# A hybrid SSM and attention encoder layer in fp32: two buffers and five renormalisations of its state stage changed

## The chip, the cores and the metric

The kernel runs as one program on one core of one Trainium2 chip. Its time is the device time of one execution, in microseconds (us); the kernel before took 918.15 us, the median of 3 executions (916.77 to 918.69). In the text PE is TensorE (matmuls and transposes), DVE is VectorE, ACT is ScalarE, POOL is GpSimd, and SP is the engine whose queue issues most DMAs. Each engine works through its own list of instructions in order; a semaphore holds an instruction back until what it needs is there.

## What is computed

One layer of an encoder for 512 tokens of width 1024, with 16 learned meta tokens in front, so L = 528 rows. All of it is float32.

```
h = rms_norm(x);  u, q, k, v, g_ssm, g_attn = split(h @ W_in)      # 512 | 1024 | 256 | 256 | 1024 | 1024
y = D * u + sum over 2 directions of Re(C x),  x[l] = lam * x[l-1] + B u[l]
                                         # 32 groups of 16 channels, 64 complex states in each
z = gelu(y);  y_ssm = z * sigmoid(z @ W_glu + b)
y_attn = attention(rope(rms_norm(q)), rope(rms_norm(k)), v)         # 16 heads, 4 KV heads
x = x + W_out(sigmoid(g_ssm) * (y_ssm @ P_ssm) + sigmoid(g_attn) * (y_attn @ P_attn))
x = x + relu(rms_norm(x) @ W1)^2 @ W2;   out = rms_norm(x)[16:]
```

`lam` = exp((a_re + i a_im) dt) is one complex number for each of 2 x 32 x 64 states. Its modulus and its phase are kept apart: the scan uses the modulus, and the phases are put on and taken off by complex rotations.

## The kernel before

Every fp32 matmul is done as three products of fp32r halves (`mm3`, L159 to L161: high by high, low by high, high by low). A weight arrives by DMA (`wf`), ACT casts it to its high half (`wh`, L98), and DVE subtracts to get the low half (`wl`, L125). PE takes 128 x 512 tiles of these products out of PSUM accumulators.

The program has stages. The first 60 us or so make the norm of x, k and v, and the small tables of the SSM on DVE (tiles `p`, 128 x 32). The **state stage** follows, from about 60 to 236 us of the span; the change lies in it alone. Behind it come the norm of k (L916 to L937), the half-GLU (L1042), attention with its query projections, the merge, W_out, and the MLP, which is by far the largest part.

The state stage treats the 32 groups in 8 runs of 4 groups, in 8-step blocks (66 columns). Directions share the partitions: 0 to 63 forward, 64 to 127 backward. Each run i has a generator `ssm_build(i)` and a generator `ssm_run(i)`:

- `ssm_build`: DVE makes the input matrices W1 (L711 to L713), PE transposes them (L720), ACT copies them out (L721). DVE makes the output matrices W2 (L728 to L733, two buffers each; the last PE reader of a buffer is the matmul `yo`, L815). The phases of the columns are the products `x1`, `x2` (L747, twice) and their sum `e` (L749); ACT copies their imaginary part as `es` (L751, L752). Then PE multiplies `kt` (L758), ACT takes most of it out (L762, L763), DVE the middle (L764, L765), and DMAs lay out the local matrix T0 (L769).
- `phase_tables`, called once in the first build that needs it, makes the powers of the phase step by doubling: a complex product (L560 to L565), then the next step is squared (`csq`) and brought back to modulus one (`renorm`: six DVE operations on 128 x 32). Three doublings serve the table of 8 entries, four that of 9.
- `ssm_run`: PE multiplies the inputs by W1 (`st`, L787), ACT copies the sums into the tile `Sx` (L789, L790), DVE rotates (L795 to L797), scans along the columns (L800, into Sx again), and rotates back; the second L797 is the last step ahead of the states. ACT copies the states into `X` (L806, L807), and PE finishes with `yo` (L813 from T0, L815 from X). After two runs PE transposes (`yt`) and ACT takes the GELU.

Two temporaries, rs1 (a piece of `gbuf`) and rs2, serve both the phase products of a build (`x1`, `x2`) and the rotations of a run (`m1`, `m2`); `Sx` is one buffer. So a build's L747 may not write rs1 before ACT has copied the states of the run before out of it (L807), and the next run's copies into Sx may not begin before the last rotation has read it.

Between the parts of these generators `pump` puts tiles of the gate projection (`gps`) and of u (`ups`) into PE's list as filler: matmuls that need none of the states. A gate tile is 24 matmuls of 128 x 512. `ssm_in` transposes u into the blocks (`up`, L672; Vc, L98; `ug`, L678; Uf, L679). The code is written in generator order, and a scheduler that simulates a timeline then fixes one order per engine, with the priorities of its own estimate; the order of the instructions is thus a result of the whole program, and an edit at one place can move instructions at another.

Of the kernel before, what the change touches and what calls it, by code (L numbers as in the profile page):

```python
# [10 lines left out]
F32 = mybir.dt.float32  # L11
# [59 lines left out]
def hybrid_block(ctx, tc, x, meta, w_in, w_glu, w_ssm, w_attn, w_out, w_m1, w_m2,  # L71
# [3 lines left out]
    V, S, Q, PE = nc.vector, nc.scalar, nc.gpsimd, nc.tensor  # L75
# [110 lines left out]
    yfl = ybuf.rearrange("p k n -> p (k n)")  # L186
# [36 lines left out]
    def ptile(pl=None, shape=(128, G), dt=F32):  # L223
        cnt[0] += 1
        return (pl or pp).tile(list(shape), dt, name=f"p{cnt[0]}")
# [269 lines left out]
    def ts(a, s1, op0, s2=None, op1=None, o=None):  # L495
        o = ptile() if o is None else o
        if op1 is None:
            V.tensor_scalar(out=o, in0=a, scalar1=s1, scalar2=None, op0=op0)
        else:
            V.tensor_scalar(out=o, in0=a, scalar1=s1, scalar2=s2, op0=op0, op1=op1)  # L500
        return o

    def stt(a, s, b, op0, op1, o=None):
        o = ptile() if o is None else o
        V.scalar_tensor_tensor(out=o, in0=a, scalar=s, in1=b, op0=op0, op1=op1)
        return o
# [52 lines left out]
    def cmul(eng, orr, oi, ar, ai, br, bi, t1_, t2_):  # L559
        eng.tensor_tensor(out=t1_, in0=ar, in1=br, op=ALU.mult)  # L560
        eng.tensor_tensor(out=t2_, in0=ai, in1=bi, op=ALU.mult)
        eng.tensor_tensor(out=orr, in0=t1_, in1=t2_, op=ALU.subtract)
        eng.tensor_tensor(out=t1_, in0=ar, in1=bi, op=ALU.mult)
        eng.tensor_tensor(out=t2_, in0=ai, in1=br, op=ALU.mult)
        eng.tensor_tensor(out=oi, in0=t1_, in1=t2_, op=ALU.add)  # L565
# [5 lines left out]
    def tz(a, b, op):  # L571
        return tt(a, b, op, o=ptile(ppz))

    def csq(r, i):
        rr = tz(tz(r, r, ALU.mult), tz(i, i, ALU.mult), ALU.subtract)
        ii = stt(r, 2.0, i, ALU.mult, ALU.mult, o=ptile(ppz))
        return rr, ii

    def renorm(r, i):
        m = tz(tz(r, r, ALU.mult), tz(i, i, ALU.mult), ALU.add)  # L580
        m = ts(m, -0.5, ALU.mult, 1.5, ALU.add, o=ptile(ppz))
        return tz(r, m, ALU.mult), tz(i, m, ALU.mult)

    wr, wi = cs, sn
    for _ in range(3):
        wr, wi = csq(wr, wi)
    wr, wi = renorm(wr, wi)
    wri = wr, wi

    def phase_tables():  # L590
        wr, wi = wri
        phase = []
        for nb in (8, 9):
            tr_ = sp.tile([128, G, nb], F32, name=f"ph{nb}r")
            ti_ = sp.tile([128, G, nb], F32, name=f"ph{nb}i")
            V.memset(tr_[:, :, 0:1], 1.0)
            V.memset(ti_[:, :, 0:1], 0.0)
            m = 1
            while m < nb:
                n = min(m, nb - m)  # L600
                bcw = [a[:, :, None].to_broadcast([128, G, n]) for a in (wr, wi)]
                s1, s2 = [a[:, :G * n].rearrange("p (g n) -> p g n", g=G) for a in (sc5, sc6)]
                cmul(V, tr_[:, :, m:m + n], ti_[:, :, m:m + n], tr_[:, :, 0:n], ti_[:, :, 0:n], bcw[0], bcw[1], s1, s2)
                m *= 2
                if m < nb or nb == 8:
                    wr, wi = renorm(*csq(wr, wi))
            phase.append((tr_, ti_))

        (pbr, pbi), (par, pai) = phase
        pa1, pa2 = [sp.tile([128, G, 2, 9], F32, name=f"pa{j}") for j in range(2)]  # L610
        S.copy(out=pa1[:, :, 0], in_=par)
        S.copy(out=pa1[:, :, 1], in_=pai)
        S.activation(out=pa2[:, :, 0], in_=pai, func=AF.Copy, scale=-1.0)
        S.copy(out=pa2[:, :, 1], in_=par)
        return pa1, pa2, pbr, pbi
# [46 lines left out]
    sw = pool(ss_st, "sw")  # L662
# [28 lines left out]
    rs1, rs2 = gfl[:, 1536:2112], sp.tile([128, 576], F32, name="rs2")  # L691
# [3 lines left out]
    def ssm_build(i8):  # L695

        gs = slice(4 * i8, 4 * i8 + 4)

        def bp(a):
            return a[:, gs, :, None].to_broadcast(W4)  # L700

        def bb(a):
            return a[:, gs, None, :].to_broadcast(W4)

        tmp = [yfl[:, 512 * j:512 * j + 512].rearrange("p (g s q) -> p g s q", g=4, s=T) for j in range(8)]

        W1T = []
        for im in range(2):
            tB, tC, tA = tmp[0], tmp[1], tmp[2 + im]
            a0, a1 = (LBr, LBi) if im == 0 else (LBi, LBr)  # L710
            V.tensor_tensor(out=tB, in0=bb(a0), in1=bp(PA[0]), op=ALU.mult)  # L711
            V.tensor_tensor(out=tC, in0=bb(a1), in1=bp(PA[1]), op=ALU.mult)
            V.tensor_tensor(out=tA[:, :, ::-1, :], in0=tB, in1=tC, op=ALU.subtract if im == 0 else ALU.add)  # L713
        yield
        for im in range(2):
            tA = tmp[2 + im]
            w1 = sw.tile([128, 4, 128], F32, tag=f"W1{im}", bufs=W1B, name="W1")
            ps = ptr("w1").rearrange("p (g n) -> p g n", g=4)
            for g in range(4):
                PE.transpose(ps[:, g, :], tA[:, g].rearrange("n s p -> n (s p)"), ident)  # L720
            S.copy(out=w1, in_=ps)  # L721
            W1T.append(w1)

        W2 = []
        for im in range(2):
            tB, tC = tmp[4], tmp[5]
            w2 = sw.tile(W4, F32, tag=f"W2{im}", bufs=2, name="W2")
            V.tensor_tensor(out=tB, in0=bb(Cr), in1=bp(PA[im]), op=ALU.mult)  # L728
            V.tensor_tensor(out=tC, in0=bb(Ci), in1=bp(PA[1 - im]), op=ALU.mult)
            if im == 0:  # L730
                V.tensor_tensor(out=w2, in0=tB, in1=tC, op=ALU.subtract)
            else:
                V.scalar_tensor_tensor(out=w2, in0=tB, scalar=-1.0, in1=tC, op0=ALU.mult, op1=ALU.subtract)  # L733
            W2.append(w2.rearrange("n g s p -> n g (s p)"))
        BP = BPs[i8 % 2]
        for hsl, csl in ((slice(0, 64), slice(0, 16)), (slice(64, 128), slice(32, 48))):
            S.copy(out=BP[hsl, :, :, csl], in_=Bb[hsl, :, gs])

        if not tables:
            tables.extend(phase_tables())  # L740
        pa1, pa2, pbr, pbi = tables
        e = sw.tile([128, 4, 2, 72], F32, tag="e", name="e")
        es = sw.tile([128, 2, 4, NC], F32, tag="es", name="es")
        E4 = [128, 4, 18, 8]
        x1, x2_ = [a.rearrange("p (g a b) -> p g a b", g=4, b=8) for a in (rs1, rs2)]
        for o, a, b_ in ((x1, pa1, pbr), (x2_, pa2, pbi)):
            V.tensor_tensor(out=o, in0=a[:, gs].rearrange("p g s a -> p g (s a)")[:, :, :, None].to_broadcast(E4),  # L747
                            in1=b_[:, gs, None, :].to_broadcast(E4), op=ALU.mult)
        V.tensor_tensor(out=e.rearrange("p g s (a b) -> p g (s a) b", b=8), in0=x1, in1=x2_, op=ALU.add)  # L749
        er, ei = e[:, :, 0, :NC], e[:, :, 1, :NC]  # L750
        S.copy(out=es[:, 0], in_=ei)  # L751
        S.activation(out=es[:, 1], in_=ei, func=AF.Copy, scale=-1.0)  # L752
        yield

        ps = ptr("kt")[:48].rearrange("p (g n) -> p g n", g=4)
        for g in range(4):
            for i in range(2):
                own = PE.matmul(out=ps[:, g, :], lhsT=BP[:, i, g, :], rhs=W2[i][:, g, :], start=i == 0, stop=i == 1)  # L758
        anchors.append(own.ins)
        pf = ps[0:16].rearrange("p g (t q) -> p g t q", t=T)  # L760
        pb = ps[32:48].rearrange("p g (t q) -> p g t q", t=T)
        S.copy(out=E[:, :, 8:15, :], in_=pf[:, :, 1:8, :])  # L762
        S.copy(out=E[:, :, 0:7, :], in_=pb[:, :, 0:7, :])  # L763
        V.tensor_tensor(out=E[:, :, 7, :], in0=pf[:, :, 0, :], in1=dd[:, gs, :], op=ALU.add)  # L764
        V.tensor_tensor(out=E[:, :, 7, :], in0=pb[:, :, 7, :], in1=E[:, :, 7, :], op=ALU.add)  # L765
        ef = E.rearrange("p g l q -> p g (l q)")
        T0 = sw.tile([128, 4, 128], F32, tag="T0", bufs=2, name="T0")
        for s in range(T):
            (nc.sync if s % 2 else nc.scalar).dma_start(out=T0[16 * s:16 * s + 16], in_=ef[:, :, (7 - s) * 16:(7 - s) * 16 + 128])  # L769
        built[i8] = W1T, W2, T0, er, es  # L770
# [5 lines left out]
    def ssm_run(i8, ws_, Uf):  # L776
        W1T, W2, T0, er, es = ws_
        gs = slice(4 * i8, 4 * i8 + 4)
        b = i8 % 2
        SX = [128, 2, 4, NC]  # L780
        S.copy(out=dec[:, :, :, 1:], in_=m8[:, None, gs, None].to_broadcast([128, 2, 4, NC - 1]))

        Sx = sw.tile(SX, F32, tag="S", name="Sx")
        for i in range(2):
            ps = ptr("st")[:, :4 * NC].rearrange("p (g n) -> p g n", g=4)
            for g in range(4):
# [56 lines left out]
    for i in range(8):  # L843
        c, b = divmod(i, 2)
# [6 lines left out]
        if i < 7:  # L851
            bg = ssm_build(i + 1)
            go(bg)
# [724 lines left out]
```

## Time and profile before

| | |
|---|---|
| time, median of 3 executions | 918.15 us (916.77 to 918.69) |
| the profiled execution's own time | 916.32 us |
| its span | 914.6 us |
| PE busy in the span | 852.6 us (93%) |
| DVE, ACT, POOL busy | 691.2, 515.9, 184.4 us |
| chain that ended last, by engine | PE 76%, DVE 14%, ACT 5% |

The profile is that of one execution. The span is the time from its first to its last recorded instruction, and the execution's time is 1.7 us longer. Busy shares are averages over all stages, so the stretches of the state stage have to be looked at by themselves. A wait is idle time of an engine ahead of an instruction, put down to the instruction that ended last of those it depends on. [...]

### The profile page before, as it was taken

The page shows a single profiled execution, that of the slowest core. Times are in us where ns is not written, and L with a number is a line of the kernel's source. Part 1 is how long each engine was busy: PE and PEld are TensorE (multiplying, and loading weights), DVE is VectorE, ACT ScalarE, POOL GpSimd, SP SyncE. Part 2 cuts the span into 40 slices and gives each one's busy share as a digit, 9 for nine tenths or more (in the row PEclk, how much of TensorE's full clock was granted, in tenths as well). Part 3 has the DMA queues.
Part 4 walks back from the last instruction along what each step waited for, and adds up shares of the span by engine and source line. Part 5 has one row for each costly group of instructions (what it writes and reads, how often), then busy time and mean ns, then how long its engine had stood idle before and what let it go on. Part 6 is the DMA issues. An engine that isn't in the chain of part 4 may idle for free.

```text
span 914.6 us, 13094 instructions
## 1 busy us (share of the span) xinstructions
PE 852.6 (93%) x4798; PEld 729.8 (80%) x4798; DVE 691.2 (76%) x1263; ACT 515.9 (56%) x908; POOL 184.4 (20%) x177
## 2 busy tenths in 40 slices
PE   6999789998999899899989999999999999999994
PEld 5998677776887789788878888888888888888884
DVE  6999999878879687867685536747667666776687
ACT  5444465555663656578785335565655555555543
POOL 1000000000111476657644432010010001000000
PEclk9999899899999999999999999999999999999997
DMA  7222202222113110002014343565656566565402
GB/s 236 71 67 67 75 13 63 75 58 65 63 47 95 50 47 24 24 24 70 2 48 137 115 138 92 187 161 138 183 138 161 140 181 153 147 180 127 109 1 92
DMA packets 96322, 88.33 MB, mean 97 GB/s; under 512 B 4337, under 2 KB 79665, under 8 KB 96258
## 3 DMA queue, kind: packets, MB, share of 16 engines
q1 hardware_dynamic: 87824, 69.25, 25.2%
q0 software_dynamic: 4016, 14.21, 7.9%
q10 hardware_dynamic: 4418, 4.04, 1.6%
q8 instruction: 38, 0.62, 0.3%
q14 instruction: 26, 0.21, 0.1%
HBM read 69.03 MB, written 2.10 MB: 78 GB/s over the span
## 4 chain that ended last, share of the span: by engine, by line
PE 76%; DVE 14%; ACT 5%; issue 2%; DMA 1%; POOL 1%; DVEq 0%; ACTq 0%; POOLq 0%
PE m L161 6%; PE m L160 6%; PE m L159 6%; PE o L159 5%; PE o L160 5%; PE o L161 5%; PE pv L1173 3%; PE sc L1099 2%; PE atr L1123 2%; DVE wl L125 2%; PE adp L159 2%; PE adp L160 2%; PE adp L161 2%; PE gps L159 2%; PE kt L758 2%
## 5 line engine op out<-in xcount | busy, mean ns | idle before, releaser
L98 ACT CAST wh<-wf 128x512 fp32r<-128x512 f32 (+1 forms) x120 | 89.8, 778 | 94.5 <-PE m L160 58.2
L1444 DVE TENSOR_TENSOR ybuf<-o,ybuf 128x1024 f32<-128x1024 f32 x52 | 63.5, 1221 | 67.9 <-PE o L161 67.8
L161 PE MATMUL m<-h2h,wl 128*128 128x512 f32 (+1 forms) x272 | 102.4, 377 | 0.8 <-DVE wl L125 0.8
L160 PE MATMUL m<-h2l,wh 128*128 128x512 f32 (+1 forms) x272 | 102.5, 377 | 0.2 <-DVE h2l L103 0.2
L159 PE MATMUL m<-h2h,wh 128*128 128x512 f32 (+1 forms) x272 | 102.3, 377 | 0.3 <-ACT h2h L98 0.2
L160 PE MATMUL o<-ol,fh 128*128 128x512 f32 (+1 forms) x216 | 83.2, 385 | 0.0
L159 PE MATMUL o<-oh,fh 128*128 128x512 f32 (+1 forms) x216 | 83.2, 385 | 0.0
L161 PE MATMUL o<-oh,fl 128*128 128x512 f32 (+1 forms) x216 | 83.2, 385 | 0.0
L125 DVE TENSOR_TENSOR wl<-wf,wh 128x512 fp32r<-128x512 f32 (+1 forms) x81 | 69.2, 873 | 14.1 <-ACT wh L98 13.3
L123 POOL DMA_DIRECT2D wl<-wf x27 | 23.4, 866 | 279.0 <-ACT wl L122 262.3
L161 PEld LDWEIGHTS m<-h2h,wl 128*128 128x128 f32 x272 | 51.2, 188 | 10.6 <-DVE wl L125 1.3
L159 PEld LDWEIGHTS m<-h2h,wh 128*128 128x128 f32 x272 | 51.1, 188 | 10.1 <-ACT h2h L98 0.5
L160 PEld LDWEIGHTS m<-h2l,wh 128*128 128x128 f32 x272 | 51.2, 188 | 9.7 <-DVE h2l L103 0.4
L1103 DVE TENSOR_REDUCE mx<-sc 128x1 f32<-128x528 f32 x64 | 44.7, 701 | 11.7 <-PE sc L1099 10.8
L103 DVE TENSOR_TENSOR pl<-atr,ph 128x512 fp32r<-128x512 f32 x64 | 43.4, 683 | 9.3 <-ACT ph L98 8.5
L98 ACT CAST ph<-atr 128x512 fp32r<-128x512 f32 x64 | 37.1, 584 | 18.1 <-PE atr L1123 17.5
L161 PEld LDWEIGHTS o<-oh,fl 128*128 128x128 f32 x216 | 40.6, 188 | 8.2
L159 PEld LDWEIGHTS o<-oh,fh 128*128 128x128 f32 x216 | 40.6, 188 | 8.1
L160 PEld LDWEIGHTS o<-ol,fh 128*128 128x128 f32 x216 | 40.6, 188 | 7.9
L804 POOL MEMSET X<- 64x8 f32 x8 | 0.9, 112 | 218.4 <-PE yo L815 218.4
L1113 POOL TENSOR_TENSOR ea<-zT,rsm 128x528 f32<-128x528 f32 x32 | 34.2, 1069 | 21.4 <-DVE rsm L1112 19.3
L1123 PE MATMUL atr<-ident,ea 128*128 128x128 f32 x192 | 36.0, 281 | 0.7 <-DVE pl L103 0.6
(403 smaller groups left out, 2523.4 us busy)
## 6 DMA issues: line engine op xcount, KB each, us to landing
wf<-in_w_in_dram SPq DMA_DIRECT2D x32, 512.0 KB, 3.9
wf<-in_w_m_dram SPq DMA_DIRECT2D x32, 512.0 KB, 4.1
q<-in_w_m_dram SPq DMA_DIRECT2D x32, 512.0 KB, 4.5
wl<-wf POOLq DMA_DIRECT2D x27, 512.0 KB, 4.4
ybuf<-in_x_dram SPq DMA_DIRECT2D x8, 512.0 KB, 3.9
wf<-in_w_attn_dram SPq DMA_DIRECT2D x8, 512.0 KB, 3.9
wf<-in_w_out_dram SPq DMA_DIRECT2D x8, 512.0 KB, 3.3
wf<-in_w_ssm_dram SPq DMA_DIRECT2D x4, 512.0 KB, 3.4
```

Source lines behind the costliest of these rows:

```text
L98: return S.copy(out=o, in_=i)
L103: b = el.tensor_tensor(out=l, in0=src, in1=h.bitcast(F32), op=ALU.subtract)
L123: Q.dma_start(out=wl[:, r], in_=wf[:, r], accum_op=ALU.add)
L125: el.tensor_tensor(out=wl[:, r], in0=wf[:, r], in1=wh[:, r].bitcast(F32), op=ALU.subtract)
L159: PE.matmul(out=o, lhsT=lh, rhs=rh, start=first, stop=False, skip_group_check=goes_on)
L160: PE.matmul(out=o, lhsT=lh, rhs=rl, start=False, stop=False, skip_group_check=goes_on)
L161: return PE.matmul(out=o, lhsT=ll, rhs=rh, start=False, stop=last, skip_group_check=goes_on)
L1103: g0 = V.tensor_reduce(out=mx, in_=sc[:, :, :NL], axis=AX.XY, op=ALU.max, negate=True)
L1113: pend.append(lambda: Q.tensor_tensor(out=en, in0=e, in1=rs_.to_broadcast([128, L]), op=ALU.mult))
L1123: PE.transpose(ps[:, j * 256 + q * 128:j * 256 + q * 128 + 128], ea[2 * f + q][:, c:c + 128], ident)
L1173: PE.matmul(out=pvt[0][:, 256 * f:256 * f + 256], lhsT=vw, rhs=pw, start=left == [8, 9], stop=left == [0, 0])
L1444: V.tensor_tensor(out=x2q[r][h], in0=z, in1=x2q[r][h], op=ALU.add)
```

## The change

Three edits, all in the state stage. Five of the six renormalisations inside `phase_tables` are left out: only the step that begins the table of 9 (after the last doubling of the table of 8) is still brought back to modulus one. The product `x1` gets a place of its own in the buffer `yfl`, past the eight temporaries of a build. `Sx` gets a second buffer.

```diff
                 m *= 2
                 if m < nb or nb == 8:
-                    wr, wi = renorm(*csq(wr, wi))
+                    wr, wi = csq(wr, wi)
+                    if m == nb:
+                        wr, wi = renorm(wr, wi)
...
-        x1, x2_ = [a.rearrange("p (g a b) -> p g a b", g=4, b=8) for a in (rs1, rs2)]
+        x1, x2_ = [a.rearrange("p (g a b) -> p g a b", g=4, b=8) for a in (yfl[:, 3072:3648], rs2)]
...
-        Sx = sw.tile(SX, F32, tag="S", name="Sx")
+        Sx = sw.tile(SX, F32, tag="S", bufs=2, name="Sx")
```

Lines behind the first edit carry numbers that are 2 higher in the changed kernel. DVE has 30 instructions fewer (25 of L492, 5 of L500); the other engines have as many as before. The order moves on PE, DVE and ACT within the state stage, and in a short piece of the MLP.

On DVE, around the first run's two rotations, there stood before (the products of the build behind it at the end, written to `gbuf`, which is rs1, and rs_888, which is rs2):

```order
L749 TENSOR_TENSOR e<-gbuf,rs_888 128x576
L795 TENSOR_TENSOR gbuf<-Sx,e 128x528
L796 TENSOR_TENSOR rs_888<-Sx,es 128x528
L125 TENSOR_TENSOR wl<-wf,wh 128x512
L797 TENSOR_TENSOR gbuf<-gbuf,rs_888 128x528
L125 TENSOR_TENSOR wl<-wf,wh 128x512
L800 SCALAR_TENSOR_TENSOR Sx<-dec,gbuf 128x528
L795 TENSOR_TENSOR gbuf<-Sx,e 128x528
L796 TENSOR_TENSOR rs_888<-Sx,es 128x528
L797 TENSOR_TENSOR gbuf<-gbuf,rs_888 128x528
L747 TENSOR_TENSOR rs_888<-pa_1116,ph8i 128x576
L747 TENSOR_TENSOR gbuf<-pa_1115,ph8r 128x576
```

and now, with x1 in `ybuf` (which is yfl):

```order
L797 TENSOR_TENSOR gbuf<-Sx,e 128x528
L749 TENSOR_TENSOR ybuf<-pa_1055,ph8r 128x576
L798 TENSOR_TENSOR rs_888<-Sx,es 128x528
L125 TENSOR_TENSOR wl<-wf,wh 128x512
L799 TENSOR_TENSOR gbuf<-gbuf,rs_888 128x528
L125 TENSOR_TENSOR wl<-wf,wh 128x512
L802 SCALAR_TENSOR_TENSOR Sx<-dec,gbuf 128x528
L797 TENSOR_TENSOR gbuf<-Sx,e 128x528
L798 TENSOR_TENSOR rs_888<-Sx,es 128x528
L799 TENSOR_TENSOR gbuf<-gbuf,rs_888 128x528
L749 TENSOR_TENSOR rs_888<-pa_1056,ph8i 128x576
L751 TENSOR_TENSOR e<-ybuf,rs_888 128x576
```

One of the next build's two products has moved ahead of the rotation's second product; the other stays behind the states.

On ACT, around the first run's copies of its states (X), there stood before:

```order
L613 ACTIVATE pa_1116<-ph9i 128x32x9
L751 COPY es<-e 128x264
L752 ACTIVATE es<-e 128x264
L98 CAST wh<-wf 128x512 x2
L366 COPY t_76<-gps 128x512
L781 COPY dec<-m_879 128x8x65
L789 COPY Sx<-st 64x264
L790 COPY Sx<-st 64x264
L789 COPY Sx<-st 64x264
L790 COPY Sx<-st 64x264
L806 COPY X<-gbuf 64x8x65
L807 COPY X<-gbuf 64x8x65
```

and now:

```order
L753 COPY es<-e 128x264
L754 ACTIVATE es<-e 128x264
L723 COPY W_1418<-w_1419 128x512
L723 COPY W_1425<-w_1426 128x512
L357 COPY uT<-ups 128x264 x2
L98 CAST wh<-wf 128x512 x2
L783 COPY dec<-m_879 128x8x65
L808 COPY X<-gbuf 64x8x65
L809 COPY X<-gbuf 64x8x65
L98 CAST wh<-wf 128x512 x2
L366 COPY t_76<-gps 128x512
```

The four copies into Sx that stood ahead of X fill the second run's Sx; they now stand eleven rows further up, ahead of the copies of the second build's `kt`, since that run has a buffer of its own. The copies of `es`, which need the first `e`, now stand ahead of the copies of a W1, of uT and of two casts of weights, which were ahead of them before.

On PE, at the fourth run's `yo`, there stood before:

```order
L758 MATMUL kt<-W_1857,BP_167 48x128
L672 MATMUL up<-ident,uT 66x128 x8
L678 MATMUL ug<-ident,Vc 128x66 x8
L815 MATMUL yo<-W_1683,X 64x128
L815 MATMUL yo<-W_1687,X 64x128
L813 MATMUL yo<-T_1754,Uf 64x128
```

and now:

```order
L817 MATMUL yo<-W_1623,X 64x128
L817 MATMUL yo<-W_1627,X 64x128
L680 MATMUL ug<-ident,Vc 128x66 x8
L826 MATMUL yt<-ident,gbuf 128x64 x8
L789 MATMUL st<-Uf,W_1779 128x66 x4
L789 MATMUL st<-Uf,W_1786 128x66 x4
```

The eight transposes `ug`, which wait for ACT's copy Vc, have moved behind this `yo`.

## Rows read from the trace of the kernel before

**Rows 1.** Busy us of each engine, share of the span, instructions

```profile
PE 852.6 (93%) x4798; PEld 729.8 (80%) x4798; DVE 691.2 (76%) x1263; ACT 515.9 (56%) x908; POOL 184.4 (20%) x177
```

**Rows 2.** Windows of the state stage (us; busy and count per engine; clock; DMA)

```profile
104.00:124.00 20.00, 11.56 (x74) 9.72 (x74) 18.30 (x28) 10.41 (x22) 0.21 (x2) 0.74 0.09 27
...
157.00:168.00 11.00, 6.84 (x38) 5.73 (x37) 9.06 (x16) 5.52 (x13) 0.21 (x2) 0.69 0.29 73
...
224.00:236.00 12.00, 7.81 (x46) 6.78 (x45) 11.20 (x16) 6.89 (x12) 1.33 (x3) 0.86 0.15 45
sum 188.00, PE 167.88 PEld 143.86 DVE 169.09 ACT 99.86 POOL 2.61; mean PE 20.99 PEld 17.98 DVE 21.14 ACT 12.48 POOL 0.33
```

**Rows 3.** Waits of PE, 48 to 236 us: total us, times, longest us

```profile
PE yo L815 <- ACT X L807: 6.6, 3, 3.5
PE yo L813 <- ACT Sx L790: 5.3, 1, 5.3
PE ug L678 <- ACT Vc L98: 2.8, 2, 2.1
```

**Rows 4.** Waits of DVE, 48 to 236 us

```profile
DVE gbuf L747 <- ACT X L807: 4.2, 5, 1.3
DVE gbuf L764 <- ACT gbuf L763: 3.3, 3, 1.8
DVE W L731 <- PE yo L815: 3.1, 3, 1.7
DVE gbuf L795 <- ACT Sx L790: 2.6, 2, 1.4
DVE st L917 <- ACT ybuf L916: 1.3, 1, 1.3
```

**Rows 5.** Timeline of PE: start us, us, instruction, count, idle before and releaser

```profile
97.19 0.39 PE L159 MATMUL gps<-hTh,wh 128*128 128x512 f32 x1
...
103.80 0.39 PE L161 MATMUL gps<-hTh,wl 128*128 128x512 f32 x1
...
111.60 0.87 PE L815 MATMUL yo<-W,X 128*64 128x128 f32 x3 [1.46 <-ACT X L807]
...
228.76 0.40 PE L815 MATMUL yo<-W,X 128*64 128x128 f32 x2 [3.52 <-ACT X L807]
...
241.26 0.39 PE L160 MATMUL adp<-zl,wh 128*128 128x512 f32 x1
```

**Rows 6.** Groups of DVE by form, 48 to 100 us: busy, mean ns

```profile
L492 DVE TENSOR_TENSOR p<-p 128x32 f32<-128x32 f32 x22 | 3.8, 182 | 0.0
```

**Rows 7.** Timeline of DVE at the renormalisations, the rotations and the stage's end

```profile
85.03 0.29 DVE L492 TENSOR_TENSOR p<-p,p 128x32 f32<-128x32 f32 x2
...
108.64 0.71 DVE L797 TENSOR_TENSOR gbuf<-gbuf,rs 128x528 f32<-128x528 f32 x1
...
225.33 1.29 DVE L125 TENSOR_TENSOR wl<-wf,wh 128x512 fp32r<-128x512 f32 x2 [0.77 <-issue]
226.54 0.70 DVE L797 TENSOR_TENSOR gbuf<-gbuf,rs 128x528 f32<-128x528 f32 x1
...
236.53 2.74 DVE L103 TENSOR_TENSOR zl<-zT,zh 128x512 fp32r<-128x512 f32 x1
```

**Rows 8.** Timeline of ACT around the first run's states

```profile
97.39 0.38 ACT L357 COPY uT<-ups 128x264 f32<-128x264 f32 x1 [1.19 <-PE ups L161]
...
102.78 0.41 ACT L751 COPY es<-e 128x264 f32<-128x264 f32 x1 [2.46 <-DVE e L749]
...
109.81 0.37 ACT L790 COPY Sx<-st 64x264 f32<-64x264 f32 x1
...
110.83 0.62 ACT L807 COPY X<-gbuf 64x520 f32<-64x520 f32 x1
```

**Rows 9.** PE in the first two runs' yo: us, busy, granted clock, DMA

```profile
111.60:116.20 4.60, 4.60 (x22) 0.50 0.00 0
123.10:125.40 2.30, 2.30 (x24) 1.00 0.03 7
```

## The prediction

> **What bounds the kernel now.** I read the busy times first, then the windows, then the waits of PE and of DVE over the state stage, then the timelines of the three engines at the places those waits named. Over the span PE is busy 93%, DVE 76% [rows 1], averages over stages with different limits that say nothing yet about this change. Inside the stage it is different. From 48 to 236 us PE works 167.88 of 188 us, DVE 169.09 [rows 2]. PE's missing 20 us are not spread out; they sit at three ends of runs. From 104 to 124 us PE is busy 11.56 of 20 us while DVE is busy 18.30, and the granted clock is 0.74; from 157 to 168 us it is 6.84 of 11 us at 0.69; from 224 to 236 us 7.81 of 12 us at 0.86 [rows 2]. At each of them the list of waits says who holds PE: `yo` waits for the states X, 6.6 us in three waits, or for ACT's copies of Sx, 5.3 us in one, and the transposes `ug` wait for Vc [rows 3]. The reader is to see that X comes from DVE's last L797, and that DVE works nearly without a break ahead of it. So the stage runs at the pace of DVE's list, and PE fills the rest of the stage with gate tiles until they run out for the moment.
>
> DVE does wait, and the reader is to see for whom: L747 waits 4.2 us in five times for the copies of X, since x1 lies where these copies read; L795 waits 2.6 us for the copies into the one Sx; L731 waits 3.1 us for `yo`, the last reader of the W2 buffer; the statistics of K, L917, 1.3 us [rows 4]. The first run shows the whole pattern. The source of X ends at 108.64 + 0.71 = 109.35 us [rows 7]. ACT's last copy into Sx runs from 109.81 us and the copies of X come behind it, the second at 110.83 us [rows 8], so X is there at 111.45 us and `yo` goes on at 111.60 us [rows 5]. The gate tile ahead of it had ended at 103.80 + 0.39 us [rows 5].
>
> [...]
>
> **The renormalisations.** Five times six operations of DVE go, 30 on 128x32. One takes 182 ns by itself [rows 6], but two of them together take 0.29 us [rows 7], so the next begins 0.11 us behind and a removed one frees about 0.10 us. That is 30 x 0.10 = 3.0 us in DVE's list ahead of the first `e`, and thus ahead of all eight runs. It is real time only if DVE isn't waiting for something else just then: between these operations stands the wait for the `kt` copies of the second build (L764, the longest 1.8 us [rows 4]). Part of the renormalisations stood ahead of it; there I take 0.4 us off.
>
> [...]
>
> **What else moves on DVE.** In the changed order a pair of `wl` subtractions that stood ahead of the last L797 comes behind it, 1.29 us for two [rows 7], 1.2 us of DVE's time; so do ten small operations of the K norm, at the same 0.10 us about 1.0 us. DVE has 3.0 + 1.2 + 1.0 = 5.2 us less to do ahead of the last states. What is moved isn't gone: some 2.1 us now come behind X. Cover: the fourth `zl` ends at 236.53 + 2.74 = 239.27 us and PE needs it at 241.26 us [rows 5, 7], so 2.0 us are hidden; if PE arrives at that place as early as X does, that cover shrinks. I charge 0.5 us.
>
> **The two buffers.** With x1 in a place of its own, one product of the next build can run beside the rotation, and L747's wait for X goes: 4.2 us at most. With two Sx the next run's copies need not wait for the last rotation, L795's 2.6 us; in the first run it also takes four copies out of ACT's way ahead of X, 0.37 us each by their row [rows 8]. The wait of L731 for `yo` isn't touched by either buffer (W2 has two, as before), but an earlier X makes an earlier `yo`; I take half, 1.5 us. L917 has moved, 1.3 us. Together 9.6 us go [rows 4].
>
> Not all of it is kept. Both products need rs2 still, so the second one can't pass the rotation. An earlier DVE meets PE's own order: the `kt` matmuls stand behind gate tiles in PE's list, and these don't get faster. At L764 of the second, sixth and eighth build DVE then waits longer: I take 0.4, 1.6 and 1.7 us, and 1.3 us for the rest, each below the longest waits of these kinds in the trace (1.8 and 1.4 us [rows 4]). That is 5.0 us back, net 4.6 us. The bounds are 0 (every removed wait returns as another) and 9.6.
>
> **ACT.** The order shows `es` ahead of two W1 copies, of uT and of two casts. Before, uT ran at 97.39 us and `es` at 102.78 us, after a wait of 2.46 us for `e` [rows 8]. With 3 us less DVE work `e` still comes some 2 to 3 us behind the place at which uT ran. The gate tile at 97.19 us [rows 5] needs its PSUM buffer emptied and its casts done by that ACT, so I expect PE to lose up to 2.8 us there. It costs nothing as long as it lies inside PE's wait for the first X (from 104.2 to 111.60 us before); if it lies outside, it costs 2.8 us. For waits of this sort that I don't see I charge 1.0 us.
>
> [...]
>
> **Sum.** 5.2 (work) + 4.6 (waits) - 0.5 - 1.0 = 8.3 us. Against the profiled execution, 916.32 - 8.3 = 908.0 us. That execution is 1.8 us below the median of the runs, so 918.15 - 8.3 = 909.9, and I say **910.0 us**. The same sum with the waits at their bounds: 3.7 us with none kept (914.4), 13.3 us with all (904.9).
>
> **Rivals.**
> Deeper, 904 us or below: the new waits don't come, and PE, no longer stopped for long at the ends of the runs, keeps the full clock there, 2.3 us at each of the first, fourth and eighth `yo`. For it: clocks of 0.74 and 0.69 in these windows [rows 2]. Against it: PE's order still has `kt` behind filler. 918.15 - 13.3 - 2.3 or less: 902 to 904 us.
>
> Only the cut: the buffers free DVE of waits that turn into waits for `kt` and W2 at once; what stays is 3.0 to 4 us: 914.5 us. For it: L731 and L764 wait in the trace already without these buffers being to blame [rows 4].
>
> No change: the stage's end is set by PE's and ACT's order, and the freed DVE time is all idle, 918 us. For it: the filler has the same total, so if PE's waits only change places nothing is won. Against it: PE is idle 20 us in a stage in which DVE isn't.
>
> Slower: ACT's queue. Where it decides is the first run: `es` and with it uT and the casts behind it; DVE has two `wl` between the first rotation's operations, which need such casts. If the casts end after about 104 us, DVE comes to these `wl` and waits, the first X is no earlier than before, and PE has lost 2.8 us at 97 us without getting it back, and a half-clock stretch more, 2.3 us [rows 9]; with waits of the later runs as before the total is 918.15 + 2.8 + 2.3 - 2 (what is left of the cut) = 921 us. For it: the strict order of ACT's list. Against it: the fewer operations ahead of `e` bring `es` forward by the same 3 us.
>
> **Chances.** The forecast's own case, 906 to 914 us, 50%; deeper 15%; only the cut 16%; no change 10%; slower 9%. The range reaches into deeper (down to 904 us) and over only the cut to the middle of no change: **904 to 918.5 us**. About 0.2%, 1.8 us, is what a measurement of this kernel can tell from no change. Faster by more: 0.79 (the first three cases, less 2 in 100 in which the cut alone ends within that); within: 0.10 (those 2 and 8 of no change); slower: 0.11 (the other 2 of no change beside the slower case).
>
> **What would show it.** In the changed profile L492 and L500 have 25 and 5 instructions fewer, and the first `e` ends 3 us or so earlier, before 100 us. L747 (now L749) waits for X no more, L795 (L797) for Sx no more. The first `yo` from X starts near 108 us instead of 111.60, the eighth near 219 to 220 instead of 228.76 [rows 5], and the wait at the fourth is gone, as `ug` is behind it. PE's idle time of 20 us in the stage falls to some 12. I am wrong if the eighth `yo` starts within 2 us of where it did, if the waits for `kt` on DVE grow by more than 9 us, or if a loss appears behind 240 us where only the K stacks, the GLU and a short piece of the MLP could differ.

## The result, and the profile after

The changed kernel took 907.14 us (median of 4 executions, 905.36 to 909.03) against 917.9 us (median of 4, 916.77 to 918.69). The ratio is 0.9884, with a 95% interval of 0.9855 to 0.9913, so 10.6 us are gone (8.0 to 13.3). The forecast was 910.0 us, 8.3 us less, in a range of 904 to 918.5. The profiled execution took 905.43 us, its span 903.5 us; the four executions lie in two pairs, 905.4 us and about 909 us, it is one of the lower pair, and why there are two is open.

All of it comes from the state stage. PE runs the same 1074 matmuls from 48 us to the end of the stage, which lies at 236.0 us before and at 225.4 us after; every matmul compared from there to the end is then 10.5 to 10.6 us earlier, so nothing is given back or won later, and the reordered piece of the MLP is worth nothing. The windows of that stretch, in the columns of [rows 2], before:

```profile
48.00:236.00 188.00, 167.88 (x1074) 143.86 (x1074) 169.09 (x356) 99.86 (x205) 2.61 (x15) 0.94 0.23 61
```

and after:

```profile
48.00:225.40 177.40, 162.74 (x1074) 138.77 (x1073) 160.83 (x315) 99.24 (x205) 2.66 (x15) 0.98 0.23 61
...
104.00:124.00 20.00, 15.64 (x112) 13.01 (x111) 19.69 (x31) 12.69 (x26) 0.43 (x4) 0.91 0.18 51
...
157.00:168.00 11.00, 11.00 (x70) 8.89 (x68) 7.52 (x13) 5.35 (x13) 0.00 (x0) 1.00 0.47 129
...
224.00:236.00 12.00, 12.00 (x57) 9.81 (x56) 11.79 (x21) 7.82 (x13) 4.37 (x1) 1.00 0.16 48
```

PE's idle time falls from 20.1 to 14.7 us, 5.5 us, and its busy time by 5.1 us with no matmul less: the granted clock, which the profile gives as a share of full speed, rises from 0.94 to 0.98. The windows at fixed times hold other work now (the last one lies behind the stage), but the `yo` of the first, fourth and eighth run, at which PE was held in [rows 2], all run at a granted clock of 1.00 (from 107.35, 153.71 and 219.47 us).

The waits of DVE after, in the columns of [rows 4]:

```profile
DVE gbuf L766 <- ACT gbuf L765: 5.5, 3, 2.9
DVE gbuf L797 <- ACT Sx L792: 5.3, 2, 3.2
DVE W L733 <- PE yo L817: 2.1, 2, 1.2
```

The product's wait for X (L747 in [rows 4], 4.2 us) is gone, and that of the K statistics (1.3 us). The wait for Sx, which the second buffer was forecast to remove, has doubled from 2.6 to 5.3 us, and that for `kt` has grown from 3.3 to 5.5 us. The waits of PE after, which answer to [rows 3]:

```profile
PE kt L760 <- DVE W L735: 3.9, 2, 2.2
PE kt L760 <- DVE W L733: 3.2, 3, 2.3
PE gps L159 <- ACT uT L357: 2.6, 2, 1.8
...
PE yo L817 <- ACT X L809: 1.6, 2, 1.2
PE ug L680 <- ACT Vc L98: 1.1, 2, 0.7
```

`yo` waits for X 1.6 us in place of 6.6, and for Sx no more (5.3 before). PE now waits for W2, which DVE makes late, and for uT. The timeline of PE after, answering to [rows 5], shows the first and the last `yo`:

```profile
99.90 0.50 PE L159 MATMUL gps<-hTh,wh 128*128 128x512 f32 x1 [1.82 <-ACT uT L357]
...
107.35 0.62 PE L817 MATMUL yo<-W,X 128*64 128x128 f32 x4 [0.37 <-ACT X L809]
...
112.20 0.42 PE L760 MATMUL kt<-W,BP 128*48 128x128 f32 x2 [2.26 <-DVE W L733]
...
219.47 0.62 PE L817 MATMUL yo<-W,X 128*64 128x128 f32 x4 [1.19 <-ACT X L809]
```

They begin at 107.35 and 219.47 us, where the forecast said near 108 and 219 to 220. ACT around the first states, answering to [rows 8]:

```profile
97.73 0.41 ACT L753 COPY es<-e 128x264 f32<-128x264 f32 x1 [3.01 <-DVE e L751]
...
98.50 1.07 ACT L723 COPY W<-w 128x512 f32<-128x512 f32 x2
99.45 0.68 ACT L357 COPY uT<-ups 128x264 f32<-128x264 f32 x2
...
105.94 0.63 ACT L808 COPY X<-gbuf 64x520 f32<-64x520 f32 x1 [1.48 <-DVE gbuf L799]
106.58 0.63 ACT L809 COPY X<-gbuf 64x520 f32<-64x520 f32 x1
```

`es` comes first and uT behind it, as the order said, and the gate tile is held 1.82 us for it. The first `e` ends at 97.70 us in place of 102.74, 5.0 us earlier where the forecast said 3. X now starts the moment its source is there.

### The profile page after: what moved, and what is told of

It is laid out like the page before. It is cut to its first block, busy times and chain, and to the rows that moved or that the text cites. A ratio compares the mean times of both kernels' runs of the same rounds, so it can differ in the third digit from the quotient of the medians.

```text
span 903.5 us, 13069 instructions
## 1 busy us (share of the span) xinstructions
PE 847.3 (94%) x4798; PEld 724.4 (80%) x4798; DVE 686.1 (76%) x1233; ACT 515.4 (57%) x908; POOL 185.6 (21%) x177
## 4 chain that ended last, share of the span: by engine, by line
PE 76%; DVE 13%; ACT 6%; issue 2%; DMA 1%; POOL 1%; ACTq 0%; SPq 0%; DVEq 0%; POOLq 0%
PE m L161 6%; PE m L160 6%; PE m L159 6%; PE o L160 5%; PE o L161 5%; PE o L159 5%; PE pv L1175 3%; PE sc L1101 2%; PE atr L1125 2%; PE adp L159 2%; PE adp L160 2%; PE adp L161 2%; PE aps L159 2%; PE aps L160 2%; PE aps L161 2%
## 5 line engine op out<-in xcount | busy, mean ns | idle before, releaser
L161 PEld LDWEIGHTS m<-h2h,wl 128*128 128x128 f32 x272 | 51.2, 188 | 10.5 <-DVE wl L125 1.3
L1105 DVE TENSOR_REDUCE mx<-sc 128x1 f32<-128x528 f32 x64 | 44.7, 702 | 12.8 <-PE sc L1101 11.9
L98 ACT CAST ph<-atr 128x512 fp32r<-128x512 f32 x64 | 37.1, 584 | 17.9 <-PE atr L1125 17.5
L1115 POOL TENSOR_TENSOR ea<-zT,rsm 128x528 f32<-128x528 f32 x32 | 34.2, 1069 | 21.4 <-DVE rsm L1114 20.1
L159 PE MATMUL gps<-hTh,wh 128*128 128x512 f32 x88 | 35.4, 403 | 2.6 <-ACT uT L357 2.6
```

The source lines that it names most:

```text
L98: return S.copy(out=o, in_=i)
L159: PE.matmul(out=o, lhsT=lh, rhs=rh, start=first, stop=False, skip_group_check=goes_on)
L161: return PE.matmul(out=o, lhsT=ll, rhs=rh, start=False, stop=last, skip_group_check=goes_on)
L1105: g0 = V.tensor_reduce(out=mx, in_=sc[:, :, :NL], axis=AX.XY, op=ALU.max, negate=True)
L1115: pend.append(lambda: Q.tensor_tensor(out=en, in0=e, in1=rs_.to_broadcast([128, L]), op=ALU.mult))
```

## The experiments

For each kernel the table gives the median, the ratio to the kernel before on the same chip with its 95% interval, and what that ratio is in us of 917. The last two columns are from the profile: DVE's busy and idle time from 48 us to the end of the last run's second L797 (L799 in the changed lines), the source of the last states.

| kernel | median us | ratio (95%) | gain us | last source ends | DVE busy / idle |
|---|---|---|---|---|---|
| before | 917.9 | 1 | | 227.2 | 160.4 / 18.9 |
| the change | 907.14 | 0.9884 (0.9855 to 0.9913) | 10.6 | 218.0 | 153.4 / 16.6 |
| e1 the cut alone | 913.11 | 0.9974 (0.9959 to 0.9989) | 2.4 | 226.2 | 156.3 / 22.0 |
| e2 x1 alone | 911.28 | 0.9946 (0.9927 to 0.9964) | 5.0 | 220.4 | 156.5 / 15.9 |
| e3 Sx alone | 921.26 | 1.0061 (1.0046 to 1.0076) | -5.6 | 233.0 | 161.8 / 23.2 |
| e4 cut and x1 | 910.23 | 0.9941 (0.9925 to 0.9957) | 5.4 | 222.2 | 153.5 / 20.7 |
| e5 x1 and Sx | 910.73 | 0.9935 (0.9917 to 0.9953) | 6.0 | 221.4 | 157.0 / 16.4 |
| e6 cut and Sx | 908.79 | 0.9906 (0.9885 to 0.9926) | 8.6 | 218.8 | 155.2 / 15.6 |
| e7 change, no sixth renorm | 908.06 | 0.9915 (0.9886 to 0.9944) | 7.8 | 218.3 | 153.8 / 16.5 |
| e8 change, three W2 | 905.13 | 0.9870 (0.9851 to 0.9889) | 11.9 | 218.7 | 153.8 / 16.8 |
| e9 old order, both buffers | 914.59 | 0.9974 (0.9961 to 0.9987) | 2.4 | 226.3 | 160.2 / 18.0 |
| e10 old order, all edits | 912.46 | 0.9963 (0.9949 to 0.9977) | 3.4 | 223.0 | 157.1 / 17.9 |
| e11 new order, renorms back | 911.30 | 0.9943 (0.9931 to 0.9955) | 5.2 | 221.8 | 158.6 / 15.2 |
| e12 new order, three W2, no sixth | 904.34 | 0.9868 (0.9851 to 0.9884) | 12.1 | 216.5 | 153.3 / 15.2 |

In twelve of the thirteen kernels the last source comes earlier (or later) by the gain (or loss) to within 2 us; in e8 it comes 8.6 us earlier and the gain is 11.9 us.

### One edit at a time, with the order that the scheduler then makes

The theory was that each edit takes its own work or wait out of DVE's list, so that the gains add up; the rivals were that one edit carries all, and that the freed time turns into waits.

**e1**: only the first hunk of the diff.

> Only the five renormalisations go; x1 and Sx as before. Theory of the path (each edit takes its own work or wait out of DVE's list): DVE's busy time ahead of the last states falls by 3.0 us if a removed operation is worth 0.10 us, by 4.9 us if it is worth 0.16 us (the groups L492 and L500 of the changed kernel against before); L747 still waits for X about 4 us; 913 to 915 us. Rival that the cut alone carries the whole change: 907 to 909 us. Rival that the freed time turns into waits: 916 to 918 us.

It gained 2.4 us. DVE's work ahead of the last states fell by 4.1 us, but its idle time grew by 3.1 us. In its trace L733 waits for `yo` 8.3 us in five times (3.1 in three before, at L731). The time is inside the 913 to 915 us that were expected, but on this chip the kernel before took 915.76 us. Both the theory and the rival that the freed time turns into waits are thus partly right: most of the freed time came back as idle time, and the wait that grew most is the one for W2's buffer.

**e2**: only `x1` to `yfl[:, 3072:3648]`. (This is not past the eight temporaries of a build, which take 4096 columns: it lies in the seventh and eighth, which no instruction of a build used.)

> Only x1 gets its own place. Theory of the path: L747's 4.2 us of waits for X go and part of it comes back as waits for kt and W2; 914 to 916 us. Rival that the cut alone carries the change: 917 to 919 us. Rival that the buffers carry it: 910 us or less.

Faster than the theory said, 5.0 us. The wait for X at the product is gone, but that at L764 grew to 6.1 us and that at L795 to 5.7 us. Still DVE's idle time ahead of the last states falls by 3.0 us, and its work by 3.8 us, which the order moved behind them, since no instruction went.

**e3**: only the second Sx. To fit, the renormalisation keeps one value in place:

```diff
-        m = ts(m, -0.5, ALU.mult, 1.5, ALU.add, o=ptile(ppz))
+        m = ts(m, -0.5, ALU.mult, 1.5, ALU.add, o=m)
```

No run shows whether this line by itself moves the order.

> Only Sx gets a second buffer; to find its space the renormalisation writes one of its intermediate values in place, with as many operations as before. Theory of the path: L795's 2.6 us of waits for Sx shrink, and the first run's X no longer stands behind four copies; 915.5 to 917.5 us. By the trace of the changed kernel, in which this wait is 5.3 us, the second buffer wins nothing: 917 to 919 us. Rival that the buffers carry the change: 912 us or less.

Slower by 5.6 us, which no theory had foreseen. The timeline of DVE in the second run shows where: between the two rotations, and even between single operations of them, stand ten products of a later build (L731, L728, L729, L713, L733, L711, L712, some twice) in place of four before, and one of them waits for `yo`:

```profile
113.47 0.71 DVE L795 TENSOR_TENSOR gbuf<-Sx,e 128x528 f32<-128x528 f32 x1
115.92 0.69 DVE L731 TENSOR_TENSOR W<-ybuf 128x512 f32<-128x512 f32 x1 [1.74 <-PE yo L815]
116.53 0.70 DVE L796 TENSOR_TENSOR rs<-Sx,es 128x528 f32<-128x528 f32 x1
...
118.35 0.70 DVE L797 TENSOR_TENSOR gbuf<-gbuf,rs 128x528 f32<-128x528 f32 x1
...
120.18 1.25 DVE L800 TENSOR_TENSOR_SCAN Sx<-dec,gbuf 128x528 f32<-128x528 f32 x1
...
125.93 0.71 DVE L797 TENSOR_TENSOR gbuf<-gbuf,rs 128x528 f32<-128x528 f32 x1
```

The second run's states are ready at 126.6 us in place of 120.9 us. Work that isn't urgent stands ahead of work that is. The wait that the buffer was made for did shrink (L795 for Sx, 2.6 to 1.3 us); the loss comes with the order that the scheduler made for this kernel.

**e4**: the change without the second Sx.

> The cut and x1's own place, Sx with one buffer. Theory of the path: the sum of both, 909 to 912 us, 2 to 4 us slower than the whole change. If the second Sx wins nothing: 907 us, as the whole change. If the three edits only work together (by the order that they make): 914 us or more.

910.23 us is inside the theory's range, but the gain, 5.4 us, is hardly more than that of x1 alone (5.0 us), where e1 and e2 add up to 7.4 us; the intervals leave either open. Since DVE's busy time equals that of the whole change to 0.1 us, the 4.2 us by which its last source is later are waiting (20.7 against 16.6 us).

### Two edits, and one step further

**e5**: the change with the five renormalisations kept (with the line of e3, for space).

> x1's own place and the second Sx, all renormalisations kept (one intermediate value written in place, as in the run with Sx alone). Theory that the second Sx only helps where x1 no longer shares rs1 with the rotation: x1 alone took 4.5 us, so 907 to 910 us here, 3 to 4 us slower than the whole change, by the cut that is missing. Rival that the second Sx costs 5 us by itself in any order: 915 us or more. Rival that the cut is what makes the second Sx useful: 911 to 913 us.

6.0 us: beside x1 the second Sx adds about 1 us, within the intervals nothing. The time is 0.7 us above the range of the theory and in that of neither rival.

**e6**: the change with `x1` still in rs1.

> The cut and the second Sx, x1 still in rs1. Theory that the second Sx only helps where x1 has its own place: 916 to 920 us, slower than the cut alone (913). Rival that the cut makes it useful: 909 us or less. L731 (L733) should wait for yo 8 us or more if the loss comes as in the run with Sx alone.

8.6 us, the opposite of the theory that the second Sx needs x1's own place: it fell. Added to the cut, Sx brings 6 us; added to nothing, it costs 5.6 us; added to x1, it brings about 1; added to both, 5 us (10.6 against e4). Effects that depend so much on each other aren't waits taken out one by one.

**e7**: the last renormalisation left out too.

```diff
-                    if m == nb:
-                        wr, wi = renorm(wr, wi)
```

> The whole change and the sixth renormalisation left out as well, so that no power of the phase is brought back to modulus one inside the tables. Six operations of DVE go, all ahead of the first e. If an operation is worth 0.10 us, DVE's busy time ahead of the last states falls by 0.6 us, if 0.16 us by 1.0 us; the time by as much if DVE's list is what counts: 905 to 907 us against 907.1 of the whole change. If the order decides: anything from 903 to 915 us, and not by the work that went.

Six operations fewer, and 908.06 us, outside the 905 to 907 us of the theory; its interval overlaps that of the change. DVE's busy time ahead of the last states rose by 0.5 us, so the order put other work there. The test doesn't tell 0.10 from 0.16 us, since the order moved.

**e8**: the change with three buffers for each W2. Space comes from two values in place (not three, as the expectation has it), the line of e3 and

```diff
-        rr = tz(tz(r, r, ALU.mult), tz(i, i, ALU.mult), ALU.subtract)
+        rr = tz(r, r, ALU.mult)
+        tt(rr, tz(i, i, ALU.mult), ALU.subtract, o=rr)
...
-            w2 = sw.tile(W4, F32, tag=f"W2{im}", bufs=2, name="W2")
+            w2 = sw.tile(W4, F32, tag=f"W2{im}", bufs=3, name="W2")
```

> The whole change with three buffers for each W2 (three intermediate values of the phase step are written in place to find the space; as many operations). The 2.1 us in which L733 waits for yo go; PE's 7.1 us of waits of kt for W2 shrink if they come from it. Theory of the path: 903 to 906 us. Rival that DVE simply reaches W2 late: kt waits as before, 906 to 908 us. Rival of the order: slower than 908 us.

905.13 us, as expected in size, but the interval overlaps that of the change and its last source is 0.7 us later; not shown to be better. W2 still waits for `yo`, 1.0 us; PE's waits of `kt` for W2 fell from 7.1 to 2.0 us, but those of `yo` for X grew from 1.6 to 10.8 us, so the order moved here too.

### The order held

After e6 the question was how much the order by itself is worth. In the last four kernels every engine's order is given: an edge of issue order alone runs from each instruction to the next, in a list taken from another kernel. In their traces PE, DVE, ACT and POOL run their instructions in just these orders:

```diff
+    for eng, runs in _ORD.items():
+        order = [k for a, n in zip(runs[::2], runs[1::2]) for k in range(a, a + n)]
+        for p, q in zip(order, order[1:]):
+            tc.add_manual_dep(seq[eng][q], seq[eng][p].name,
+                              mybir.DependencyInfo(mybir.DependencyClass.NoSync, mybir.DependencyReason.DATA),
+                              reason="pin")
```

**e9**: the order of before, both buffers, all renormalisations. x1 lies at `yfl[:, 3328:3904]`: at 3072 it shares 256 columns with the temporary of the K norm (L907), which in the old order comes ahead of the last build's x1.

> Both buffers, all renormalisations kept, and every engine's order held at that of the kernel before (added edges of issue order alone; x1 at yfl[3328:3904], which no K norm writes, since at 3072 that order is impossible). So only waits can change. Theory that waits count by themselves: L747's 4.2 us for X and part of L795's 2.6 us go, DVE's idle time ahead of the last states falls from 18.9 us to 14 to 16; 2 to 5 us faster than before. Rival that the gain comes from the new order: within 1.5 us of before.

2.4 us (1.2 to 3.6), which fits the theory and doesn't exclude its rival. DVE's idle time ahead of the last states is 18.0 us, where the theory had 14 to 16. The waits of DVE, 48 to 236 us:

```profile
DVE gbuf L764 <- ACT gbuf L763: 4.7, 4, 1.8
DVE W L731 <- PE yo L815: 4.6, 4, 1.7
DVE gbuf L795 <- ACT Sx L790: 2.6, 2, 1.4
```

L747's 4.2 us are gone, but L764 has 1.4 and L731 1.5 us more, so 2.9 of them came back. The wait for Sx is 2.6 us, the same as before [rows 4]: in this order the second Sx does nothing for the wait it was made for. What it does free is ACT: before, ACT's copies into Sx waited 1.2 us in two times for the rotation that still read it (L796), and here they don't.

**e10**: the same with the cut.

> All three edits with the order of the kernel before held (less the 30 operations; x1 at yfl[3328:3904]). Theory that work and waits count by themselves: another 3 to 5 us below the run with the old order and the buffers alone, 6 to 10 us faster than before. Rival that the gain comes from the new order: 0 to 3 us faster than before, as with the cut alone (2.7 us).

3.4 us (2.1 to 4.7). All three edits without the new order give a third of the gain. That is 0.4 us past the 0 to 3 us of the rival that the gain comes from the order; the interval excludes the 6 to 10 us of the theory that work and waits count by themselves. What the added edges cost by themselves was not run; e12, which has them too, isn't slower than the change. What the cut adds here shows in the windows of DVE (us, busy, clock, DMA), in e9

```profile
48.00:226.20 178.20, 160.18 (x347) 0.95 0.23 61
```

and in e10

```profile
48.00:223.00 175.00, 157.12 (x315) 0.97 0.23 62
```

as 3.1 us of work and 3.2 us of time on DVE.

**e11**: the order and the buffers of the change, the five renormalisations back, each behind its squaring.

> The changed kernel with its order held and the five renormalisations put back, each behind its squaring. Buffers and order are those of the change, so the difference to it is the work of 30 operations of DVE: 3 us (0.10 us each), 5 us (0.16 us each), or about 0 where DVE would only have waited: 910, 912, or 907 us.

5.2 us faster than before, so the 30 operations cost 5.4 us in this order by the ratios (4.2 by the medians). DVE's busy time ahead of the last states is 158.6 against 153.4 us, 5.2 us more for 30 operations. In the traces the last source comes 3.9 us later, as 1.4 us of waiting went; the time by itself, 911.30 us, lies between the 910 and 912 us of the two prices. The timeline shows one renormalisation:

```profile
87.07 0.30 DVE L492 TENSOR_TENSOR p<-p 128x32 f32<-128x32 f32 x2
87.40 0.19 DVE L492 TENSOR_TENSOR p<-p,p 128x32 f32<-128x32 f32 x1
87.62 0.18 DVE L500 TENSOR_SCALAR p<-p 128x32 f32<-128x32 f32 x1
87.84 0.30 DVE L492 TENSOR_TENSOR p<-p,p 128x32 f32<-128x32 f32 x2
88.05 0.69 DVE L711 TENSOR_TENSOR ybuf<-LBi,PA 128x512 f32<-128x512 f32 x1
```

Six operations take 0.98 us, 0.16 each. The two that don't need each other start 0.1 us apart (0.30 us for both, 0.18 to 0.19 for one); one that needs the last starts 0.22 us behind it. In the order of before, others stood between most of them, and the starts lay 0.10 to 0.12 us apart (83.71 to 84.59 us), but not everywhere: the pair of [rows 7] at 85.03 us itself starts 0.22 us behind the operation that it needs, and that one 0.22 us behind the one that it needs.

```profile
84.59 0.19 DVE L492 TENSOR_TENSOR p<-p,p 128x32 f32<-128x32 f32 x1
84.81 0.18 DVE L500 TENSOR_SCALAR p<-p 128x32 f32<-128x32 f32 x1
85.03 0.29 DVE L492 TENSOR_TENSOR p<-p,p 128x32 f32<-128x32 f32 x2
```

**e12**: the order of the change held, three W2 and the sixth renormalisation out.

> The changed kernel with its order held, the sixth renormalisation left out and three buffers for each W2 (intermediate values of the phase step in place). With the order held nothing can be lost by it: L733's 2.1 us of waits for yo go, and 0.6 to 1.0 us of work; by the path 904 to 906 us against 907.1. If DVE waits for something else there instead: 907 us.

904.34 us, inside what was expected. W2's waits for `yo` are gone, but DVE's busy time is only 0.1 us less, where 0.6 to 1.0 us were expected. Its ratio of 0.9868 lies below that of the change, with intervals that overlap; it beats the kernel before by 12 us, and isn't shown to beat the change.

## Why the prediction was right

The time, the direction and the place were right. That 910.0 came so near to 907.14 us is in part luck: the work was put 1.8 us too low, the waits 2.3 us too high, 1.5 us of charges didn't come, and 1.3 us were won behind the last source, which no term had. None of the signs of being wrong appeared: the eighth `yo` starts 9.3 us earlier, the waits for `kt` on DVE are 5.5 us in all, and nothing is lost behind 240 us. By its steps:

**The bound.** That DVE's list sets the stage's pace held: the last source came 9.3 us earlier, the last `yo` 9.3 us, the end of the stage 10.6 us, and in the table gain and last source go together.

**DVE's work, forecast 5.2 us less, measured 7.0 us** (160.4 to 153.4). L492 and L500 took 3.5 us less ahead of the last states, when overlapped time is counted once; ten K norm operations 1.2 us (forecast 1.0), the pair of `wl` 1.1 us (1.2). The other 1.2 us are spread over many operations. The price of 0.10 us was right for the old order only: there the cut is worth 3.1 us on DVE (e10 against e9), in the new order 5.2 us (e11). The row from which it was read is a pair of operations that don't need each other; the rows just ahead of it, 0.22 us apart, show the other price. In e11, too, an operation that needs the last one starts 0.22 us behind it, where that one's recorded length is 0.18 to 0.19 us.

**DVE's waits, forecast 4.6 us less net, measured 2.3 us** (18.9 to 16.6). This is the term that was mis-sized. The step "with two Sx the next run's copies need not wait for the last rotation, L795's 2.6 us" failed: the wait is 5.3 us after, and with the order held (e9) 2.6 us, the same as before. What L795 waits for is ACT's copy of PE's sums, and where that copy stands in ACT's list isn't changed by a buffer alone. The longest of these waits after, at 166.17 us, shows it: PE's sums (`st`) were there by 160.0 us, but ACT's list had four DMA issues of T0 ahead of the copies, which lasted until 163.9 us.

```profile
158.02 2.00 PE L789 MATMUL st<-Uf,W 128*128 128x66 f32 x16
...
159.55 4.36 ACTq L771 DMA_DIRECT2D T<-gbuf  x4
...
164.59 0.38 ACT L791 COPY Sx<-st 64x264 f32<-64x264 f32 x1 [5.35 <-DMA T<-gbuf]
...
166.17 0.71 DVE L797 TENSOR_TENSOR gbuf<-Sx,e 128x528 f32<-128x528 f32 x1 [3.25 <-ACT Sx L792]
```

The other waits came near: L747's 4.2 us went, L917's 1.3 us went, L731 lost 1.0 us (1.5 forecast), and L764 gained 2.2 us (3.7 forecast for three `kt`).

**ACT and the charge behind X.** The gate tile lost 1.82 us for uT at 99.90 us (forecast: up to 2.8 us), as the order said. Yet the 1.0 and 0.5 us that I charged don't show: from the last source to the end of the stage the gain grew by 1.3 us.

**The clock.** The forecast kept it for the deeper rival, at 2.3 us for each `yo`, the 4.60 less the 2.30 us of [rows 9]. It came with the main case: the first 22 matmuls of `yo` took 4.60 us at 0.50 [rows 9], and after

```profile
107.35:109.94 2.59, 2.59 (x22) 1.00 0.00 0
```

That is 2.0 us less. PE had waited 0.37 us ahead of this `yo`, where before it had waited 5.27 and 1.46 us; that shorter waits spare the lower clock was the prediction's estimate, which no run tests by itself. The clock's share of the 10.6 us is 5.1 us of PE's busy time; the two views count the same gain, PE's once as idle and clock, DVE's once as work and waits, and can't be added.

**What the working didn't separate.** It read the new order for what stands where, and priced the moved `wl` and K norm. It didn't ask what the edits are worth if the order stays. They are worth 3.4 us (e10); the other 7 us (0.9963 against 0.9884) come only with the new order. Of these the DVE columns of the table show 3.7 us of work that no longer stands ahead of the last states (157.1 to 153.4) and 1.3 us of waiting (17.9 to 16.6); the stage's end adds the rest. Why the same second Sx is worth 6 us beside the cut and -5.6 us alone is put down to the order, which is shown at one place in e3 and for the whole change in e10; which rule of the scheduler makes it so was not tried. The opposite control, the order of the change with the buffers of before, can't exist: ACT would fill the second run's Sx ahead of `es`, which the first run's rotations still need before that Sx is free. It stays open how far the order of before could be made better without any of the three edits.

**The rivals.** "Slower by ACT's queue" had its cause (es ahead of uT) and not its effect: the first X came 3.4 us earlier at its source. "The cut alone carries it" is out (e1). "No change" is out by the interval, which begins 8.0 us below. "Deeper" was right about the clock and wrong about the waits: PE's idle time in the stage is 14.7 us, where the main case had some 12.

## What to carry to other kernels

Where a scheduler orders the whole program, an edit is two things, the wait or work that it takes away and the order that it brings about, and the second can be the larger: hold the old order and run the edit in it, and hold the new order and take the edit out. A buffer frees an instruction only if its last reader is what it waits for; look at who ends the wait, not at which tile it is for. What a small DVE operation costs depended here on whether its neighbour needs its result, 0.2 against 0.1 us (e11); read the price from a row of the same kind.

## What the runs showed that was not expected

The deeper rival kept the full clock where PE isn't stopped for long. But PE at 112.20 us of the changed kernel had waited 2.26 us, and the eight transposes behind that ran at a granted clock of 0.58 on the mean (112.55 to 114.30 us): 1.75 us for eight, against 1.03 us at 1.00 for eight at 92.43 us. In the trace of before, too, the `yo` of the fourth run stood at 0.50 behind waits of 2.13 and 1.67 us.

```profile
92.43 1.03 PE L722 MATMUL w<-ident,ybuf 128*128 128x128 f32 x8
...
112.55 1.75 PE L722 MATMUL w<-ident,ybuf 128*128 128x128 f32 x8
```
